# RMSNorm with SiLU: a last block scaled inside the activation, with its squares moved ahead and one store at its end

## The chip, the cores and the metric

The kernel runs on one core of one Trainium2 chip. The metric is the device time of one execution in microseconds (us). A profiled execution gives a span, which runs from the first to the last instruction and is about 2 us shorter than the time. A DMA is a transfer between the chip's memory (HBM, where inputs and outputs lie) and SBUF (the core's working memory); the profile counts 16 DMA engines, fed here from two queues: loads are issued by ScalarE (q10, 67.11 MB), stores by SyncE (SP, q1, 67.12 MB with the load of gamma).

## The reference

```python
# x: 8 x 1024 x 2048 float32, gamma: 2048, eps: 1e-5
rms = np.sqrt(np.mean(x ** 2, axis=-1, keepdims=True) + eps)
out = gamma * x / rms
return (out * (1 / (1 + np.exp(-out)))).astype(np.float32)      # SiLU
```

## The kernel before

The 8192 rows are cut into 16 blocks of 512 rows. A block is a tile of 128 partitions with J = 4 rows of 2048 elements in each: 4.19 MB. Six buffers go round. For each block, ScalarE and VectorE share the sums of squares (two rows each, for some blocks one and three), ScalarE takes the root, VectorE inverts it to rstd and multiplies by rstd and gamma in one instruction per row, ScalarE does SiLU in two halves, and SP stores the block.

```python
    def multiply(b):
        for j in range(J):
            nc.vector.scalar_tensor_tensor(out=row(b, j), in0=row(b, j), scalar=rstds[b][:, j:j + 1],
                                           in1=g, op0=ALU.mult, op1=ALU.mult)

    def silu(b, halves=False):
        for h in range(0, J, 2):
            cols = slice(h * d, (h + 2) * d)
            nc.scalar.activation(out=blocks[b][:, cols], in_=blocks[b][:, cols], func=ACT.Silu)
            if halves:
                nc.sync.dma_start(out=ob[b][:, cols], in_=blocks[b][:, cols])
        if not halves:
            store(b)
    # ... cut: loads, squares, root, invert
        for b in range(last):                    # last = 15
            # ... cut: two branches for the earlier blocks
            else:                                # b == 14
                multiply(b)
                silu(b)
                squares_scalar(b + 1)
                squares_vector(b + 1)
                root(b + 1)
            invert(b + 1)
        multiply(last)
        silu(last, halves=True)
```

The timeline shows each engine run its instructions in the order written here, with waits for tiles that another engine writes: the first Silu half of block 15, at 296.90 us, waits 3.59 us for VectorE's multiply.

## Time and profile before

| | before |
|---|---|
| time, median of 6 runs | 317.20 us (316.82 to 317.46) |
| span of the profiled run | 315.1 us |
| moved by DMA | 134.2 MB, 426 GB/s over the span |
| busy share: VectorE, ScalarE | 75%, 68% |
| store of block 14: issued, landed | 286.5, 304.5 us |
| last two half stores issued | 300.55 and 305.07 us |
| last half landed (end of SP's wait) | about 314.0 us |

An instruction's times are read from the timeline. A store has two: its issue, and its landing, where the profile has the transfer complete. Between them lie the wait in the queue behind earlier stores and the transfer itself: 18.0 us for block 14 here. The landing of the last store, near 314.0, is the last wait ahead of the span's end at 315.1. The view of the DMA queue's own waits shows this as the longest wait of SP's last instruction (engine and line, what it waited for: us in total, times, longest):

```profile
SPq L184 <- DMA out_dram<-xt: 8.6, 1, 8.6
```

A half of 2.1 MB needs less than 5 us at 426 GB/s, and the wait is 8.6.

### The profile page before, as it was taken

To read this page: it belongs to the slowest core of one execution; us is meant where nothing else is said; L and a number is where in the kernel's file an instruction comes from. 1 tells how busy PE (TensorE), PEld (TensorE's weight loads), DVE (VectorE), ACT (ScalarE), POOL (GpSimd) and SP (SyncE) were. 2 spreads that over 40 slices of the span, in tenths; PEclk is the share of its full clock that TensorE was granted. 3 is DMA by queue.
4 is the path that set the end of the run, shared out by engine and by line. 5 is a ranking of instruction groups with operands and counts; after the bars stand their busy time and mean duration, and the time that the engine had idled before them with its cause. 6 is when DMAs were issued, how large, how long until landed. Compare 5 with 4: busy or idle time off the path is not lost.

```text
span 315.1 us, 436 instructions
## 1 busy us (share of the span) xinstructions
PE 2.1 (1%) x8; PEld 0.5 (0%) x8; DVE 235.8 (75%) x157; ACT 213.4 (68%) x134; POOL 0.2 (0%) x4
## 2 busy tenths in 40 slices
PE   0200000000000000000000000000000000000000
PEld 0000000000000000000000000000000000000000
DVE  0679597979995695957969489593995939994920
ACT  1349998972799258682687727877288768779560
POOL 0000000000000000000000000000000000000000
DMA  8999999999999999999999999999999999999997
GB/s 334 399 466 399 399 466 399 466 404 462 412 454 408 454 412 453 412 453 412 453 420 445 428 437 433 433 433 433 445 420 445 424 441 424 445 420 453 412 426 306
DMA packets 4763, 134.24 MB, mean 426 GB/s; under 512 B 533, under 2 KB 533, under 8 KB 537
## 3 DMA queue, kind: packets, MB, share of 16 engines
q10 hardware_dynamic: 2304, 67.11, 49.7%
q1 hardware_dynamic: 2456, 67.12, 49.4%
q14 instruction: 3, 0.02, 0.0%
HBM read 67.12 MB, written 67.11 MB: 426 GB/s over the span
## 4 chain that ended last, share of the span: by engine, by line
DMA 68%; DVE 18%; ACT 8%; issue 1%; DVEq 1%; ACTq 0%
DMA xt<-in_x_dram 68%; DVE xt L93 14%; DVE junk_v L74 4%; ACT xt L99 4%; ACT junk_a L66 2%; ACT L83 1%; DVEq L184 1%; ACT L99 0%; ACT rms L83 0%; DVE rstd L88 0%; DVE ss L74 0%; ACTq L55 0%; ACTq L83 0%; DVEq L74 0%
## 5 line engine op out<-in xcount | busy, mean ns | idle before, releaser
L93 DVE SCALAR_TENSOR_TENSOR xt<-xt,rstd,g 128x2048 f32<-128x2048 f32 x64 | 146.2, 2347 | 0.2
L99 ACT ACTIVATE xt<-xt 128x4096 f32<-128x4096 f32 x32 | 115.6, 3616 | 33.6 <-DVE xt L93 33.5
L74 DVE CUSTOM_DVE_ANT_0 junk_v<-xt 128x2048 f32<-128x2048 f32 x37 | 85.1, 2300 | 42.3 <-DMA xt<-in_x_dram 41.6
L66 ACT ACTIVATE junk_a<-xt 128x2048 f32<-128x2048 f32 x27 | 50.6, 1875 | 20.8 <-DMA xt<-in_x_dram 20.5
L83 ACT ACT_TABLE_LOAD x15 | 19.2, 1283 | 27.5 <-DVE ss L74 27.4
L99 ACT ACT_TABLE_LOAD x15 | 19.2, 1283 | 0.3
L88 DVE RECIPROCAL rstd<-rms 128x4 f32<-128x4 f32 x16 | 2.8, 173 | 12.9 <-ACT rms L83 12.9
L121 DVE COPY g<-junk_v 128x2048 f32<-128x2048 f32 x1 | 2.3, 2291 | 9.4 <-PE junk_v L119 9.4
L83 ACT ACTIVATE rms<-ss,eps_t 128x4 f32<-128x4 f32 x16 | 4.8, 297 | 5.7 <-DVE ss L74 5.5
L74 DVE DVE_READ_ACCUMULATOR2_ANT ss<- 128x1 f32 x37 | 5.2, 141 | 0.0
L66 ACT ACTIVATION_READ_ACCUMULATOR junk_a<-xt 128x1 f32 x27 | 5.0, 186 | 0.0
L114 ACT ACT_TABLE_LOAD x1 | 1.3, 1283 | 3.8 <-issue 3.8
L119 PE MATMUL junk_v<-grow,ones 1*128 1x512 f32 x8 | 2.1, 1133 | 8.2 <-DMA grow<-in_gamma_dram 8.2
L112 DVE MEMSET ones<- 128x128 f32 x1 | 0.2, 165 | 0.8 <-PEq L170 0.8
L119 PEld LDWEIGHTS junk_v<-grow,ones 1*128 1x128 f32 x8 | 0.5, 307 | 8.2 <-issue 8.2
L114 ACT ACTIVATE junk_a<-ones 128x1 f32<-128x1 f32 x1 | 0.2, 174 | 0.0
L170 POOL MEMSET const-bfloat16-1.0<- 128x1 bf16 x1 | 0.1, 101 | 0.0
L170 POOL MEMSET const-uint8-127<- 128x1 uint8 x1 | 0.1, 101 | 0.0
L170 POOL MEMSET const-float32-0.0<- 128x1 f32 x1 | 0.1, 98 | 0.2 <-issue 0.2
L170 POOL MEMSET const-float32-1.0<- 128x1 f32 x1 | 0.1, 98 | 0.0
L113 DVE MEMSET eps_t<- 128x1 f32 x1 | 0.1, 59 | 0.0
## 6 DMA issues: line engine op xcount, KB each, us to landing
xt<-in_x_dram ACTq DMA_DIRECT2D x16, 4096.0 KB, 38.7
out_dram<-xt SPq DMA_DIRECT2D x15, 4096.0 KB, 29.8
out_dram<-xt SPq DMA_DIRECT2D x2, 2048.0 KB, 8.8
grow<-in_gamma_dram SPq DMA_DIRECT2D x1, 8.0 KB
```

Source lines behind the costliest of these rows:

```text
L66: nc.scalar.activation(out=junk_a, in_=row(b, j), func=ACT.Square, accum_out=sss[b][:, j:j + 1])
L74: nc.vector.tensor_tensor_reduce(out=junk_v, in0=row(b, j), in1=row(b, j), scale=1.0, scalar=0.0, op0=ALU.mult, op1=ALU.add, accum_out=sss ...
L83: nc.scalar.activation(out=rms, in_=sss.pop(b), func=ACT.Sqrt, scale=1.0 / d, bias=eps_t)
L88: nc.vector.reciprocal(out=rstd, in_=rmss.pop(b))
L93: nc.vector.scalar_tensor_tensor(out=row(b, j), in0=row(b, j), scalar=rstds[b][:, j:j + 1], in1=g, op0=ALU.mult, op1=ALU.mult)
L99: nc.scalar.activation(out=blocks[b][:, cols], in_=blocks[b][:, cols], func=ACT.Silu)
L112: nc.vector.memset(ones, 1.0)
L114: nc.scalar.activation(out=junk_a[:, 0:1], in_=ones[:, 0:1], func=ACT.Square)
L119: nc.tensor.matmul(junk_v[:, c * w:(c + 1) * w], ones[k:k + 1, :], grow[k:k + 1, :], start=True, stop=True)
L121: nc.vector.tensor_copy(out=g, in_=junk_v)
L170: nc = _bacc.Bacc("TRN2", target_bir_lowering=False, num_devices=1)
L184: with _tile.TileContext(nc) as tc:
```

## The change

The intent is a shorter tail of compute. VectorE multiplies the last block by gamma alone, which needs no rstd and so can start before the root is known; rstd goes in as the scale that the Silu instruction applies to its input. The squares of block 15 on ScalarE go ahead of block 14's Silu. The last store is one transfer in place of two halves.

```diff
             else:
                 multiply(b)
+                squares_scalar(b + 1)
                 silu(b)
-                squares_scalar(b + 1)
                 squares_vector(b + 1)
                 root(b + 1)
-            invert(b + 1)
-        multiply(last)
-        silu(last, halves=True)
+            if b + 1 < last:
+                invert(b + 1)
+
+        for j in range(J):
+            if j == J // 2:
+                invert(last)
+            nc.vector.tensor_mul(out=row(last, j), in0=row(last, j), in1=g)
+        for j in range(J):
+            nc.scalar.activation(out=row(last, j), in_=row(last, j), func=ACT.Silu,
+                                 scale=rstds[last][:, j:j + 1])
+        store(last)
```

The cut part of the diff takes the `halves` argument out of `silu`.

More of the change, by code (lines that the diff above doesn't have):

```diff
@@ L94, in multiply, with silu @@
                                            in1=g, op0=ALU.mult, op1=ALU.mult)
-    def silu(b, halves=False):
+    def silu(b):
         for h in range(0, J, 2):
@@ L99, in silu @@
             nc.scalar.activation(out=blocks[b][:, cols], in_=blocks[b][:, cols], func=ACT.Silu)
-            if halves:
-                nc.sync.dma_start(out=ob[b][:, cols], in_=blocks[b][:, cols])
-        if not halves:
-            store(b)
+        store(b)
     def store(b):
```

## The prediction

> **What bounds the kernel now.** I read the page first: the span, then the row of DMA shares in 40 slices, then the bytes over the whole span.
>
> ```profile
> span 315.1 us, 436 instructions
> ...
> DMA  8999999999999999999999999999999999999997
> GB/s 334 399 466 399 399 466 399 466 404 462 412 454 408 454 412 453 412 453 412 453 420 445 428 437 433 433 433 433 445 420 445 424 441 424 445 420 453 412 426 306
> ...
> HBM read 67.12 MB, written 67.11 MB: 426 GB/s over the span
> ```
>
> The reader is to see that the DMA engines are at 90% or more in every slice but the first and the last, at the same rate whatever the compute engines do, while the page has VectorE busy for 75% and ScalarE for 68% of the span. The bytes (each element read once, written once) are not touched by the change.
>
> The change works on the last blocks only, where a compute tail might still be exposed. So next I took the timeline of the end. In it ScalarE's last Silu halves and the stores issued behind them are:
>
> ```profile
> 282.86 3.62 ACT L99 ACTIVATE xt<-xt 128x4096 f32<-128x4096 f32 x1 [0.91 <-DVE xt L93]
> ...
> 292.26 9.14 DVE L93 SCALAR_TENSOR_TENSOR xt<-xt,rstd,g 128x2048 f32<-128x2048 f32 x4
> 296.90 3.62 ACT L99 ACTIVATE xt<-xt 128x4096 f32<-128x4096 f32 x1 [3.59 <-DVE xt L93]
> 300.55 4.86 SPq L101 DMA_DIRECT2D out_dram<-xt  x2
> 301.43 3.62 ACT L99 ACTIVATE xt<-xt 128x4096 f32<-128x4096 f32 x1 [0.91 <-DVE xt L93]
> ```
>
> Block 14's Silu ends and its store is issued at 286.5; block 15's two half stores are issued at 300.55 and 305.07. Asked transfer by transfer, the stores of blocks 13, 14 and the first half of 15 took 17.5, 18.0 and 8.8 us from issue to landing (issued at 277.22), so they landed at 294.7, 304.5 and 309.35; the end of the program waited 8.6 us more after the last issue (its own line among the waits of the DMA queue), which puts the last landing at 314.0. Thus 4.19 MB landed every 9.8 us and each half 4.6 to 4.9 us after the one before: they land one behind another at full rate, never at a distance set by their issues. The windows of the tail say how much was left to move, the last number being GB/s:
>
> ```profile
> 290.00:292.00 2.00, 0.00 (x0) 0.00 (x0) 0.00 (x0) 1.97 (x4) 0.00 (x0) 1.00 1.10 475
> ...
> 298.00:300.00 2.00, 0.00 (x0) 0.00 (x0) 2.00 (x2) 2.00 (x1) 0.00 (x0) 1.00 1.14 492
> 300.00:302.00 2.00, 0.00 (x0) 0.00 (x0) 1.40 (x1) 1.09 (x2) 0.00 (x0) 1.00 0.72 311
> 302.00:304.00 2.00, 0.00 (x0) 0.00 (x0) 0.00 (x0) 2.00 (x1) 0.00 (x0) 1.00 0.99 426
> ...
> 312.00:314.00 2.00, 0.00 (x0) 0.00 (x0) 0.00 (x0) 0.00 (x0) 0.00 (x0) 1.00 0.44 188
> ```
>
> The six windows from 302 to 314 (426, 467, 393, 418, 467, 188) add up to 2 us x 2359 = 4.72 MB. Block 15 is 128 x 8192 x 4 bytes = 4.19 MB, so 0.52 MB of block 14 were still to go at 302, until about 303.2 at 426 GB/s. The six from 290 to 302 (475, 492, 328, 492, 492, 311) add 5.18 MB; together 9.90, minus two blocks (8.39), leaves 1.51 MB of block 13 at 290, until about 293.1. This takes stores to be served in order, as their landings suggest. So at the end the **store backlog** binds, not ScalarE or VectorE. The view of the chain that ended last follows Silu and VectorE there, because it follows releases; it does not show that a released store then stood behind another.
>
> [...]
>
> **The change, part by part.**
>
> *Squares ahead of Silu 14.* ScalarE is free of block 13 at 273.60 + 3.62 = 277.22. The load of block 15 was issued at 240.36 and took 38.7 us, so it is there at 279.06. Two squares with their accumulator reads took 263.75 - 259.70 = 4.05 us for block 14, so now they run from 279.1 to 283.15. Silu 14 follows, both halves ready by then (VectorE ends its multiply at 282.84): two halves back to back took 7.12 us for block 0, so it ends at 290.3. Store 14 is issued at 290.3, not 286.5: **3.8 us later**. But block 13's bytes occupy the engines until about 293.1, 2.8 us after that. In the start of the trace the first load, issued at 0.73, moves bytes within the window from 1 to 2 us, so a store needs about 1 us to start. Cost on the path: 0, with 1.8 us of margin.
>
> *Root and table loads.* VectorE's squares of block 15 end at 287.4 as before. The root waits for Silu 14: load 1.28, Sqrt 0.30, so 290.3 to 291.9, then the Silu load to 293.2. Before, the same three ended at 293.3. No gain, no loss.
>
> *Multiply by gamma alone.* Four fused multiplies of 2347 (9.4 us of busy time) become four products[...]. Two of them no longer wait for rstd: they run from 287.4 to 292.0, in the time in which VectorE was idle (4.56 us in front of the reciprocal). The reciprocal takes 0.2, the others end at 294.5 and 296.8.
>
> *Silu with rstd as its scale.* Two Silus of 3617 (7.23 us) become four[...]. They begin with the table load's end at 293.2, not 296.9, and are not held by VectorE (row 3 starts at 298.9, its product is ready at 296.8). The end is near 300.9, where it was 305.05: **the compute tail is 4.1 us shorter.**
>
> *One store in place of two.* It is issued at 300.9, 4.1 us ahead of the second half before, 0.35 us behind the first. Block 14's bytes end at about 303.2, so with 1 us to start it is queued 1.3 us before its turn. Its 4.19 MB then take as long as before: full stores landed 9.8 us apart, the two halves together 9.5 (314.0 - 304.5). So one transfer costs between 0 and 0.3.
>
> The sum on the path: 0 (store 14) + 0 (the shorter tail, hidden behind the backlog) + about 0.15 (the middle of the last) gives a span near 315.2. Run time stood 2.1 above the span as a median (317.2 against 315.1), so about **317.3**. Against that, the window 300 to 302 is the one thin place of the tail (311 where 426 is the mean, a lack of 0.23 MB or 0.5 us): if part of it was idle engines and goes away, up to 0.5 is gained, which I count half. I predict **317.1**.
>
> **The rivals.**
> 1. *The compute tail is the bound*, as the chain of waits has it: then 4.1 us fewer would be gained. Speaks against it: even with empty queues a 4.19 MB store issued at 300.9 would need its 9.7 us or so and about 1 us to start, hence 311.6 at best plus a completion of about 0.7 (bytes end near 313.3 before, landing 314.0): 312.3, so at most 1.7 us less, 315.5. And bytes of block 14 are queued until 303.2.
> 2. *The delayed store 14 opens a gap*, so that engines run dry between stores 13 and 14. A new wait in place of the old. For it: 1.8 us of margin is thin if some of the 16 engines run ahead of the mean; the windows show only the mean. Against it: the same holds for store 15 before, with 1.7 us of margin, and cost at most 0.5. Would give 317.5 to 318.5.
> 3. *ScalarE becomes the bound*: [...]the tail starts 3.7 earlier. To delay the last store beyond its turn the rows would have to be 0.3 us longer each. It would give some tenths.
>
> **Range and chances.** From 315.5 (rival 1 in full) to 318.5 (rival 2 in full) is all that I can construct. The three runs before lie within 0.22. I put 8 in 10 on 316.2 to 318.0. Two per cent is 6.3 us; no rival reaches a third of it, so within 2% has 0.98 and each side 0.01.
>
> **What would show it.** In the changed profile: store 14 issued near 290.3 but landing still near 304.5 (14 us from issue in place of 18.0); [...]one store of block 15, 13 us from issue to landing, landed near 314; DMA shares still at 9 up to the last slice[...]. Wrong would be the backlog step if store 14 lands later than 305.5 (a gap) or the last store lands before 313 (the tail did bind). The whole is wrong if the change altered the DMA rate of the 280 us ahead of the tail, which nothing in the diff touches.

The sum on the path came to a span of 315.2 us and a time of 317.3, and the forecast to 317.1. The sum of the compute tail: from the table load's end at 293.2 it came to 298.9 for the start of row 3 and 300.9 for its end, so 7.7 us for four rows were the estimate. In the trace before, the two Silu halves of block 0 took 7.12 us for as many elements, which alone would give 300.3. The products' ends at 294.5 and 296.8: with the 2347 ns measured for the fused multiply, counted from 287.4, they are 294.6 and 297.0, and still ahead of the Silu rows.

## The result, and the profile after

| | before | after |
|---|---|---|
| time, median of 6 runs | 317.20 us | 316.99 us (316.69 to 317.69) |
| ratio, 95% interval | | 0.9999 (0.9986 to 1.0012) |
| span of the profiled run | 315.1 us | 315.1 us |
| store 14 issued, landed | 286.5, 304.5 | 290.3, 304.6 |
| compute ends | 305.05 | 300.87 |
| last landing (end of SP's wait) | about 314.0 | about 314.0 |

A ratio is the mean time of one kernel's runs over that of the other's in the same rounds, so it is not quite the ratio of the two medians. The result is no change, at a resolution of 0.13%.

The view of a store's issue and landing gives 300.90 + 13.4 = 314.3 for the last landing of the changed kernel. It has no value for the last store of the kernel before, so the two are compared by SP's wait. The timeline of the changed kernel's tail (start, us, engine, line and operation; a number in brackets would be idle time in front):

```profile
283.16 7.11 ACT L99 ACTIVATE xt<-xt 128x4096 f32<-128x4096 f32 x2
...
287.48 4.49 DVE L155 TENSOR_TENSOR xt<-xt,g 128x2048 f32<-128x2048 f32 x2
290.28 1.28 ACT L83 ACT_TABLE_LOAD   x1
291.58 0.30 ACT L83 ACTIVATE rms<-ss,eps_t 128x4 f32<-128x4 f32 x1
291.89 1.28 ACT L157 ACT_TABLE_LOAD   x1
...
293.19 7.68 ACT L157 ACTIVATE xt<-xt,rstd 128x2048 f32<-128x2048 f32 x4
```

The compute did what was intended. ScalarE has no gap from 279.22 to 300.87: the 3.59 us and 0.91 us of waiting for VectorE, which the brackets of the timeline before showed, are gone. Compute ends 4.2 us earlier, and the span is the same. The groups of the page show the prices of the two new instructions (mean ns behind the busy time):

```profile
L155 DVE TENSOR_TENSOR xt<-xt,g 128x2048 f32<-128x2048 f32 x4 | 8.9, 2279 | 0.0
L157 ACT ACTIVATE xt<-xt,rstd 128x2048 f32<-128x2048 f32 x4 | 7.7, 1990 | 0.0
```

And the waits of the DMA queue show where the 4.2 us went:

```profile
SPq L190 <- DMA out_dram<-xt: 12.8, 1, 12.8
```

SP waits 12.8 us for the last landing, where it waited 8.6. The time saved in front of the last issue is spent again behind it. The page's row of DMA shares is as full as before:

```profile
DMA  8999999999999999999999999999999999999996
```

### The profile page after: what moved, and what is told of

Same layout as the page of the kernel before. It is cut to its first block, busy times and chain, and to the rows that moved or that the text cites. A ratio compares the mean times of both kernels' runs of the same rounds, so it can differ in the third digit from the quotient of the medians. Undisturbed runs are those within 1.5% of the kernel's fastest.

```text
span 315.1 us, 436 instructions
## 1 busy us (share of the span) xinstructions
PE 2.1 (1%) x8; PEld 0.5 (0%) x8; DVE 235.3 (75%) x157; ACT 213.8 (68%) x136; POOL 0.2 (0%) x4
## 4 chain that ended last, share of the span: by engine, by line
DMA 68%; DVE 14%; ACT 11%; issue 2%; ACTq 1%; DVEq 0%
DMA xt<-in_x_dram 68%; DVE xt L93 9%; DVE junk_v L74 5%; ACT xt L99 4%; ACT junk_a L66 3%; ACT xt L157 2%; ACT L83 1%; ACTq L190 1%; ACT L157 0%; ACT L99 0%; ACT rms L83 0%; DVE ss L74 0%; DVE rstd L88 0%; ACTq L55 0%; ACTq L83 0%
## 5 line engine op out<-in xcount | busy, mean ns | idle before, releaser
L93 DVE SCALAR_TENSOR_TENSOR xt<-xt,rstd,g 128x2048 f32<-128x2048 f32 x60 | 137.0, 2347 | 0.1
L99 ACT ACTIVATE xt<-xt 128x4096 f32<-128x4096 f32 x30 | 108.3, 3615 | 27.2 <-DVE xt L93 27.1
L155 DVE TENSOR_TENSOR xt<-xt,g 128x2048 f32<-128x2048 f32 x4 | 8.9, 2279 | 0.0
L157 ACT ACTIVATE xt<-xt,rstd 128x2048 f32<-128x2048 f32 x4 | 7.7, 1990 | 0.0
```

Of the source, the lines that this page charges most:

```text
L155: nc.vector.tensor_mul(out=row(last, j), in0=row(last, j), in1=g)
L157: nc.scalar.activation(out=row(last, j), in_=row(last, j), func=ACT.Silu, scale=rstds[last][:, j:j + 1])
```

## The experiments

**Theory.** Near the end the stores stand one behind another, each landing about 9.8 us after the one ahead. An issue can then move by as much as it stands ahead of its turn, and nothing is seen. **Rival A, cancellation:** the shorter tail gained up to 4 us and waiting for the whole block before storing it took them back. **Rival B:** the later store of block 14 cost something, hiding a gain. Eleven kernels were run, each in 3 rounds or more beside the kernel before.

### One transfer alone, and two halves with the new tail

The two halves of rival A, taken apart. The first kernel is the one before, with this edit:

```diff
-        silu(last, halves=True)
+        silu(last)
```

> The kernel before with one change: block 15 is stored by one transfer after its second Silu. Backlog theory: the store is issued at 305.1, some 1 us to start, so it moves from 306.1, where block 14's bytes ended at 303.2; the engines idle 2.9 us, the last landing moves from 314.0 to about 316.9, time near 320.0 (+0.9%). Rival, one transfer is free by itself because a store's landing is hidden anyway: 317.2. Rival, the compute tail binds and the change is a cancellation of two opposite parts: the single store must then cost what the shorter tail gains, about +4.1, 321.3.

Measured: 318.82 us against 317.09, ratio 1.0051 (1.0038 to 1.0064). So with the old, longer tail one transfer does cost 1.7 us. The store is issued at 305.09 and lands 11.1 us later, at 316.2. The direction is the theory's, the size is not: 2.9 were expected.

The second kernel is the changed one, with its store cut in two:

```diff
             nc.scalar.activation(out=row(last, j), in_=row(last, j), func=ACT.Silu,
                                  scale=rstds[last][:, j:j + 1])
-        store(last)
+            if j % 2 == 1:
+                cols = slice((j - 1) * d, (j + 1) * d)
+                nc.sync.dma_start(out=ob[last][:, cols], in_=blocks[last][:, cols])
```

> The changed kernel with its last store cut into two halves, the first issued after row 1 (near 297.1), the second near 300.9, both 3.5 to 4.2 us ahead of the halves of before. Backlog theory: both wait for block 14's bytes until 303.1; no gain, 316.8 to 317.2, last landing near 314.0. Rival, cancellation (the shorter tail is worth up to 4.1 and the single transfer took it back): 313 to 315.5.

Measured: 317.06 us against 317.09, ratio 1.0000 (0.9987 to 1.0012). The halves are issued at 296.93 and 300.72, over 3.6 us ahead of the halves of before, and nothing comes of it (the profiled run was the slowest of its six, at 317.96; its stores of blocks 13 and 14 both landed about 1 us later than usual, at 295.9 and 305.6, so it had lost that time ahead of the last block's stores; the other five lie from 316.84 to 317.31). Rival A in its plain form falls: if the new tail had gained anything that the single transfer took back, this kernel would show it. The first kernel tells what the single transfer needs: it is free here because the shorter tail issues it early enough (300.90 in place of 305.09).

### How much the last store may be late

One and three idle Silus of 2048 elements are put ahead of the four last Silus; they read gamma and write a scratch tile, so the output stays right.

```diff
+        for _ in range(N):            # N = 1, 3
+            nc.scalar.activation(out=junk_a, in_=g, func=ACT.Silu)
         for j in range(J):
             nc.scalar.activation(out=row(last, j), in_=row(last, j), func=ACT.Silu,
```

> The changed kernel with one idle Silu of 2048 elements (about 1.8 us) ahead of the four last ones. The last store is issued near 302.7 in place of 300.9. Backlog theory: it starts near 303.7 against a turn at 303.1, so 1.3 us of the 1.8 are hidden and 0.5 us show: 317.5. Rival, the tail binds: +1.8, 318.8.

> The same with three idle Silus (about 5.4 us): last store issued near 306.3. Backlog theory: 1.3 us hidden, 4.1 show: 321.1. Rival, the tail binds: +5.4, 322.4. Rival, the tail is hidden altogether: 317.0. The two late runs give the slope and so the slack in front of the last store.

Measured: 316.97 us (ratio 0.9994, 0.9981 to 1.0007) and 320.24 us (1.0096, 1.0081 to 1.0111), against 317.09. The last store is issued at 302.65 and 306.40, in place of 300.90. So 1.75 us of delay cost nothing, and 5.5 us cost 3.2. If what lies past the slack shows in full, about 2.3 us are hidden, not 1.3; one point past the slack does not show that slope by itself, but the landings below give the same 2.3. The windows of the slower one show the idle DMA engines themselves (last two columns: DMA share and GB/s):

```profile
302.00:304.00 2.00, 0.00 (x0) 0.00 (x0) 0.00 (x0) 2.00 (x2) 0.00 (x0) 1.00 0.50 213
304.00:306.00 2.00, 0.00 (x0) 0.00 (x0) 0.00 (x0) 2.00 (x2) 0.00 (x0) 1.00 0.00 0
306.00:308.00 2.00, 0.00 (x0) 0.00 (x0) 0.00 (x0) 0.37 (x1) 0.00 (x0) 1.00 0.61 262
```

This is what a gap looks like, and neither the kernel before nor the changed one has it.

The same slack can be read from landings alone. The view of a store gives the time from issue to landing; here for the last store of the slower run, for the last store and store 14 of the changed kernel, and for store 14 of the kernel before:

```profile
DMA to landing us min/median/max: 11.1/11.1/11.1
DMA to landing us min/median/max: 13.4/13.4/13.4
DMA to landing us min/median/max: 14.3/14.3/14.3
DMA to landing us min/median/max: 18.0/18.0/18.0
```

With an empty queue the store of a block lands 11.1 us after its issue (in this run, and in four others told here). In the changed kernel the last store takes 13.4 us, so 2.3 are queue.

### Why the slack was mis-sized

The prediction placed the end of block 14's bytes from the GB/s of the windows. The slow run has a store that moves alone, in which one can see what that view records. First its transfers from 306 to 318.4, in 40 slices of 0.31 us each:

```profile
DMA  0009900990099009900990097009200900000000
GB/s 0 0 0 529 1163 0 0 740 951 0 0 740 951 0 0 740 951 0 0 1057 634 0 0 1374 317 0 0 1586 106 0 0 1691 0 0 0 0 0 0 0 0
DMA packets 144, 4.19 MB, mean 338 GB/s; under 512 B 16, under 2 KB 16, under 8 KB 16
```

The bytes come in eight lumps about 1.2 us apart, with nothing between them. Of 144 packets 16 are small; the other 128 carry 4.19 MB, so 32 KB each, or eight for each of 16 engines if they share evenly. In slices of 0.30 us, the one from 310.90 to 311.20 has a busy share of 4.06, which no busy time within it can give, and the slices beside it have 0.00: the view puts all bytes and all time of a packet at one point. Three more views tell which point. They are the share of the 16 engines' time that one lump takes (the slow run, window 307 to 308, last column), the 16 small packets at the end of the same store (316.9 to 317.2), and the 16 small packets at the end of block 14 in the kernel before (303.2 to 304.15):

```profile
q1 hardware_dynamic: 16, 0.52, 121.9%
DMA packets 16, 0.00 MB, mean 0 GB/s; under 512 B 16, under 2 KB 16, under 8 KB 16
DMA packets 42, 0.43 MB, mean 448 GB/s; under 512 B 16, under 2 KB 16, under 8 KB 16
```

The 16 packets of a lump take 121.9% of 1 us, so 1.22 us each, all of it booked in one window (which is also why a window's DMA share can be above 1.00). That is the distance between lumps, so packets follow each other without a gap, at 0.52 MB in 1.22 us or 430 GB/s. The last lump lies in the slice near 315.7; the small packets come 1.2 us later, near 317.0, and the landing is at 306.40 + 11.1 = 317.5. So a lump marks the start of a packet, and the small packets mark the end of a store's data. An end that one reads from these windows is then early by up to one packet, 1.2 us, about the amount by which both slacks were too small (1.0 here, 1.4 for store 14 below). In the kernel before, the small packets of block 14 are spread from 303.2 to 304.1, just ahead of its landing at 304.5: the prediction's 303.2 is when the first of the engines was done, and the last was done 0.9 us later.

### Rival B: is it the later store of block 14?

First the reordering alone, on the kernel before:

```diff
                 multiply(b)
-                silu(b)
                 squares_scalar(b + 1)
+                silu(b)
                 squares_vector(b + 1)
```

> The kernel before with the two ScalarE squares of block 15 ahead of block 14's Silu, nothing else. Store 14 is issued near 290.3 in place of 286.5, the reciprocal stays near 292.0, the last halves are issued at 300.6 and 305.1 as before. Backlog theory: store 14 still lands near 304.5, time 317.2 (within 0.3). Rival, the later store 14 opens a gap: +0.5 to +1.5.

Measured: 316.93 us against 316.99, ratio 0.9999 (0.9984 to 1.0014). Store 14 is issued at 290.6 and takes 14.3 us. Then the new tail without the reordering: the changed kernel with halves stored as above, and

```diff
                 multiply(b)
-                squares_scalar(b + 1)
                 silu(b)
+                squares_scalar(b + 1)
                 squares_vector(b + 1)
```

> Gamma alone with rstd as Silu's scale, in four rows, and halves stored, but with block 14's Silu ahead of the squares as in the kernel before. Store 14 issued near 286.5; Silu rows from 293.3 to 301.0. Backlog theory: 317.0, last landing near 314.0, though the compute tail is 4 us shorter. Rival, the shorter tail is worth something once store 14 is not delayed: 313 to 315.5.

Measured: 316.94 us, ratio 0.9999 (0.9982 to 1.0015). The reordering neither costs nor gains, with either tail; the four Silu rows run from 293.42 here and from 293.19 in the changed kernel. Last, its slack: two and four idle Silus between the squares of block 15 and the Silu of block 14, in the changed kernel with halves stored.

```diff
                 squares_scalar(b + 1)
+                for _ in range(N):    # N = 2, 4
+                    nc.scalar.activation(out=junk_a, in_=g, func=ACT.Silu)
                 silu(b)
```

> The changed kernel with halves stored and two idle Silus (3.6 to 3.8 us in all) ahead of block 14's Silu, so that store 14 is issued near 294.0 while the last halves keep slack. Backlog theory: block 13's bytes end at 293.1, the store starts near 295.0, so 1.8 us of slack are used up and the engines idle about 1.9 us: 318.9, store 14 landing near 306.4. Rival, no margin at all: +3.7, 320.7. Rival, hidden: 317.0.

> The same with four idle Silus (about 7.4 us): store 14 issued near 297.7, starts near 298.7, idle about 5.6 us: 322.6. Rival, no margin: +7.4, 324.4. If the slope between the two early runs is near 1 us per us, the slack in front of store 14 is read from them.

Measured: 317.75 us (ratio 1.0021, 1.0007 to 1.0036) and 321.67 us (1.0146, 1.0131 to 1.0161). Store 14 is issued at 294.01 and 298.08, and in both runs lands 11.1 us later, which is the time with an empty queue. Between the two runs 4.07 us of delay add 3.9 us of time, so past the slack it goes one to one. In the changed kernel the store takes 14.3 us, so its slack is 3.2 us; the change used 3.8 us of some 7 that were there before (18.0 - 11.1). Rival B falls for the change, and shows itself where the delay is made larger. The windows of the run with four idle Silus:

```profile
292.00:294.00 2.00, 0.00 (x0) 0.00 (x0) 0.08 (x1) 2.00 (x1) 0.00 (x0) 1.00 0.65 279
294.00:296.00 2.00, 0.00 (x0) 0.00 (x0) 0.00 (x0) 2.00 (x2) 0.00 (x0) 1.00 0.00 0
296.00:298.00 2.00, 0.00 (x0) 0.00 (x0) 0.00 (x0) 2.00 (x1) 0.00 (x0) 1.00 0.00 0
298.00:300.00 2.00, 0.00 (x0) 0.00 (x0) 0.31 (x2) 1.95 (x4) 0.00 (x0) 1.00 0.61 262
```

The lumps of block 13 end soon after 293, as the prediction had it from a sum of bytes; but a lump is a packet's start, so the block's last packets took 1.2 us more, and that is the slack that the prediction missed.

### The same tails with the backlog taken away

If the backlog is what hides the gain, taking it away must bring the gain out. In three kernels the store of block 14 is left out, so their output is wrong (that block is never written). They move 4.19 MB less and are compared with each other only.

```diff
     def store(b):
+        if b == nblk - 2:
+            return
         nc.sync.dma_start(out=ob[b], in_=blocks[b])
```

> Wrong on purpose: the kernel before without the store of block 14, so that the queue has nothing ahead of block 15's store after about 293.1. Here the compute tail does bind. Halves issued at 300.6 and 305.1: the first moves from 301.6 to 306.4, the second from 306.4 to 311.2, landing near 311.9, time near 315.1. (It moves 4.19 MB less, so it is to be compared with the other clear runs only.)

> Wrong on purpose: the changed kernel without the store of block 14. Its one store is issued near 300.9, moves from 301.9 to 311.6, lands near 312.3, time near 315.5: as slow as the cleared kernel before or slower by some tenths, because waiting for all four rows gives back what the shorter tail gained. Rival, the shorter tail as such is worth 4 us: 311.

> Wrong on purpose: as the run before, but with block 15 stored in two halves, issued near 297.1 and 300.9. First half moves from 298.1 to 302.9, second from 302.9 to 307.7, landing near 308.4, time near 311.6: 3.5 us less than the cleared kernel before. If so, the change of the multiply is worth over 3 us in a kernel whose queue is empty at the end, and the backlog alone hides it here. If the three clear runs agree, the reason is something else than the backlog.

| tail, without the store of block 14 | last issue | issue to landing | time, median |
|---|---|---|---|
| of before, two halves | 305.46 | 6.6 | 314.51 us |
| changed, one store | 301.05 | 11.1 | 314.63 us |
| changed, two halves | 300.85 | 7.4 | 310.93 us |

With an empty queue the new tail is worth 314.51 - 310.93 = 3.6 us if the store stays in halves. The reordering of the squares is in this number; with the backlog in place it moved the start of the Silu rows by 0.2 us (293.42 and 293.19 above). With one store they are worth nothing, since the transfer of the whole block takes 11.1 us where the last half takes 6.6. Here rival A holds: the change contains two parts that cancel in a kernel whose queue runs empty. In the kernel with its backlog the new tail gains nothing where the halves stay (317.06), so there is no gain for one store to cancel; one store costs 1.7 us only with the old tail, which issues it 1.9 us past the slack (305.09 against 300.90 + 2.3). The windows of the first and the second show the empty queue:

```profile
298.00:300.00 2.00, 0.00 (x0) 0.00 (x0) 2.00 (x2) 2.00 (x1) 0.00 (x0) 1.00 0.00 0
300.00:302.00 2.00, 0.00 (x0) 0.00 (x0) 1.77 (x1) 1.09 (x2) 0.00 (x0) 1.00 0.31 131
```

```profile
298.00:300.00 2.00, 0.00 (x0) 0.00 (x0) 0.00 (x0) 2.00 (x2) 0.00 (x0) 1.00 0.00 0
300.00:302.00 2.00, 0.00 (x0) 0.00 (x0) 0.00 (x0) 1.02 (x1) 0.00 (x0) 1.00 0.57 246
```

The expectations for these three runs were 0.6 to 0.9 us too high, all in the same direction; the difference of 3.5 us between the first and the third was right. These three tails are the ones measured with the backlog in place, where they gave 317.20, 316.99 and 317.06; what differs is whether another store stands in the queue ahead of the last one. No correct version was faster than the two kernels beyond noise: each of the four that kept ahead of the queue lies within 0.1% of the kernel before, and its interval includes 1.

## Why the prediction was right

The time was predicted at 317.1 us, and 316.99 was measured. That the two agree to 0.1 us is partly luck: the sum on the path gave 317.3, and 0.2 of the difference came from the thin window below, which held no gain; the six runs themselves spread over 1.0 us. That the change is worth nothing was no luck. By its steps:

- **The store backlog binds: right, and shown.** The tail became 4.2 us shorter without a change of the time; the idle Silus cost nothing up to the slack and one to one after it; without the backlog the shorter tail is worth 3.6 us.
- **Store 14 issued 3.8 us later at no cost: right.** It was to be issued at 290.3 and to land near 304.5, and it was issued at 290.3 and landed at 304.6. Its margin was put at 1.8 us and is 3.2.
- **The compute tail ends near 300.9: right.** It ends at 300.87. A Silu row took 1990 ns (7.68 us for the four) and a product by gamma 2279. VectorE's busy time fell by 0.5 us, and ScalarE's rose by 0.4, sizes without weight.
- **"queued 1.3 us before its turn": mis-sized.** It is 2.3 us. The term was the end of block 14's bytes, read from windows that put a packet's 0.5 MB (over 16 engines) at its start. The error was on the safe side, so the total stood. The same term made the expectation for one transfer with the old tail 1.2 us too high, and those for the three slower delayed runs too high by 0.9 to 1.2 (317.5 for the fastest one was 0.5 too high).
- **One transfer costs 0 to 0.3: right in this tail**, where the last landing stayed at about 314.0. It is no property of the transfer: with the old tail it cost 1.7 us.
- **The thin window from 300 to 302 might give up to 0.5 us: wrong.** It is there after the change as well (344 GB/s in that window, 311 before), and swings of this size come with the lumps of 0.5 MB (the windows of 2 us from 290 to 300 swing from 328 to 492 before). With the same bytes and the same end, nothing shows idle time in it that the change could have won.
- **Rival 1 at most 1.7 us less: too small as a bound, and never reached.** With nothing queued ahead, one store issued at 301.05 ended the kernel at 314.63, which is 2.4 us less than 316.99, about the slack of 2.3. With the backlog, even the kernel with the new tail and halves stayed at 317.06.

## What to carry to other kernels

Before shortening a tail, compare the time that the last store takes to land with the time in an empty queue: the difference was the slack here (13.4 - 11.1 = 2.3 us). As long as there is some, shortening the tail by any amount gained nothing here, and lengthening it within the slack cost nothing (1.75 us of delay: 316.97 us). The chain of waits follows who released an instruction and does not show that a released transfer stood behind another, so the landings of the last few stores, one by one, are the better view (the chains ended in Silu at 305.05 and 300.87, with the last landing near 314.0 in both kernels). A change that pairs an earlier finish with a larger last transfer should be judged part by part, as one can pay for the other where the queue does run empty (314.51 and 314.63 us above).
